# Transposing the dense stages of an encoder trunk: the residual stream as channels by tokens, weights stationary

## The chip, the cores and the metric

The kernel runs on one core of a Trainium2 chip, as one program. The metric is the device time of one execution in microseconds (us). Three runs of the kernel before took 1546.14, 1547.98 and 1548.44 us. A profiled execution took 1544.88 us. In names used below, PE is the matmul engine, PEld its weight load, DVE the vector engine, ACT the activation engine, POOL the GpSimd engine, and SP the engine that issues most transfers.

## What is computed

Two layers work on a stream x of 1024 tokens by 1024 channels in float32. Each layer normalises x, projects it to queries, keys, values and a gate, mixes tokens (layer 0, mixer A: attention over a neighbourhood of a 16 x 64 grid; layer 1, mixer B: attention over all tokens, 16 query heads and 4 key heads, with rotary positions), multiplies by the gate and projects back. Then a second input p is projected and added under a gate:

```python
for i in range(DEPTH):
    h = rms_norm(x, norm_g[i])
    ...
        y = mixer_a(h, a_w_in[j], a_rpb[j], a_w_out[j])
    ...
    x = x + y
    g = jax.nn.sigmoid(rms_norm(x, ple_norm_g[i]) @ ple_w_gate[i])
    x = x + g * (p[i] @ ple_w_proj[i])
return rms_norm(x, final_norm_g)
```

`rms_norm(x, g)` is x times a factor per token, 1/sqrt(mean(x^2) + eps), times a gain g per channel. A mixer ends with `(o * silu(gate)) @ w_out`.

## The kernel before

**Stages.** The program runs mixer A, dense stage 0, mixer B and dense stage 1. A dense stage (`dense_phase(l)`) has two passes. The pass "out" is the output projection plus residual; the pass "ple" is the gate projection, tanh, product with the projected p and residual. In dense stage 1 the pass "ple" ends with the final norm and the store of the result.

**Three products for one.** Every float32 operand is kept as a high part and a low part of a reduced format, and each product is three matmuls (`split3`, all recorded at L317 through `mm`): high by high, high by low, low by high. The activations of the current stage are in `HTh` and `HTl`, as [channel in chunk, token tile, channel chunk, token]: 128 partitions are channels, so they can be either operand of a matmul. There are 8 token tiles of 128 tokens (`NT`) and 8 channel chunks of 128 (`KC`).

**Orientation.** `proj_T` makes an output of channels by tokens: the weight block is stationary, HTh/HTl move with 512 tokens. The mixers use it for queries, keys and gates in A and for gates in B. `proj_N` makes tokens by channels: a token tile of HTh/HTl is stationary and the weights move. Mixer B uses it with 256 columns for q, k and v, and the dense passes use it with 512 columns. A dense pass goes over two halves of the output channels (`hf`), and in each over the 8 token tiles: 24 matmuls of 128x512 to one tile and half, issued as two parts of 12. The very last tile of the last pass is made in two halves of 256 columns.

**Norm and turn.** The residual stream is in eight tiles `X[t]`, tokens by channels. After each half, ACT squares the tile with a running sum (L1282, L1291). When the second half of two tiles is there, `norms` makes the factor (DVE L411, POOL's power L325) and multiplies the tile by factor and gain (DVE L421, 1024 wide). `to_ht` then transposes the product on PE, in groups of four 128x128 transposes into a PSUM bank (L427), and ACT and DVE copy it into HTh and HTl (L428, L429). These groups wait in a list `pend` and one is issued between two parts of 12 matmuls; the last ones of dense stage 0 are issued in mixer B's opening, between its first projections (`pre` in `mixer_b`). In the final pass `norms` writes the result, which SP stores (L1299, L1302).

**Weights.** `Weights` is a queue of units of 128 x 1024 elements. SP loads a unit into one of two staging tiles (L205), ACT writes its high part (L220) and DVE its low part (L221). `pulse` or `WQ.pump` moves it one step after each part: a unit is split at the earliest 3 steps after its load was issued, and the next load is issued at the earliest 3 steps after a split. A dense pass uses eight units, four for each half of the channels; the first half's come from pool 1 (`wp1`, four slots), the second half's from pool 2 (`wp2`, four slots). A unit holds two of the 8 input chunks for 512 output channels. `hold` keeps the staging tiles free while the last normalised tiles use them.

**Order in the mixers.** `mix` interleaves attention steps with projection parts by given costs, and two lists of postponed work (`post`, `later`) tick with it. In mixer B all projections share one PSUM bank after the opening (`pd`, one buffer). Its gate leaves PSUM by an ACT copy (L523); mixer A's gate leaves by a DVE product with `R`, the norm factor per token spread over all partitions (L525), since A's activations are x times gain without the factor. The projected p (`pp_items`, L548) goes to memory in the mixers and comes back in the pass "ple" (`load_pp`, L1258).

## Time and profile before

| | us |
|---|---|
| runs shown | 1546.14, 1547.98, 1548.44 |
| profiled execution | 1544.88 |
| its span, first to last instruction | 1543.1 |
| mixer A with start-up | 0 to 524.8 |
| dense stage 0 | 524.8 to 713.6 |
| mixer B, opening and attention | 713.6 to 1351.3 |
| dense stage 1 to its last matmul | 1351.3 to 1535.6 |
| rest | 1535.6 to 1543.1 |

A line of the profile names the source line, the engine, the operation, output<-inputs by tile name and their shapes, then "x" and the count; behind the bar are the busy time, the mean duration of one in ns, and the idle time before them with what ended it. The duration of a matmul is from its start to its modelled end and overlaps the next one, so the pace is read from starts or from a whole stretch. In the chain of waits a line gives start, length, engine, tile and line.

### The profile page before, as it was taken

The page shows a single profiled execution, that of the slowest core. Times are in us where ns is not written, and L with a number is a line of the kernel's source. Part 1 is how long each engine was busy: PE and PEld are TensorE (multiplying, and loading weights), DVE is VectorE, ACT ScalarE, POOL GpSimd, SP SyncE. Part 2 cuts the span into 40 slices and gives each one's busy share as a digit, 9 for nine tenths or more (in the row PEclk, how much of TensorE's full clock was granted, in tenths as well). Part 3 has the DMA queues.
Part 4 walks back from the last instruction along what each step waited for, and adds up shares of the span by engine and source line. Part 5 has one row for each costly group of instructions (what it writes and reads, how often), then busy time and mean ns, then how long its engine had stood idle before and what let it go on. Part 6 is the DMA issues. An engine that isn't in the chain of part 4 may idle for free.

```text
span 1543.1 us, 24012 instructions
## 1 busy us (share of the span) xinstructions
PE 1513.8 (98%) x9016; PEld 1324.3 (86%) x9016; DVE 963.5 (62%) x1638; ACT 847.5 (55%) x1696; POOL 350.6 (23%) x468
## 2 busy tenths in 40 slices
PE   8999999999999999999999999999999999999998
PEld 8789888988988788888988889989899888788886
DVE  4675676566576435556867776677777877624533
ACT  7564555455466423333467676767767767622422
POOL 1231232223122010000432233545041300000124
PEclk9999999999999999999999999999999999999999
DMA  7211312221124961232210111102111213651213
GB/s 300 79 61 47 96 50 67 68 73 60 62 78 124 352 220 44 89 130 79 85 36 22 39 60 41 51 25 69 40 31 42 76 46 118 225 200 55 71 59 130
DMA packets 85635, 138.97 MB, mean 90 GB/s; under 512 B 12816, under 2 KB 49808, under 8 KB 85520
## 3 DMA queue, kind: packets, MB, share of 16 engines
q1 hardware_dynamic: 80912, 122.77, 24.0%
q10 hardware_dynamic: 4608, 14.68, 2.7%
q8 instruction: 71, 1.16, 0.3%
q14 instruction: 44, 0.36, 0.1%
HBM read 104.80 MB, written 32.62 MB: 89 GB/s over the span
## 4 chain that ended last, share of the span: by engine, by line
PE 84%; DVE 6%; ACT 5%; issue 3%; DMA 1%; POOL 1%; ACTq 0%; POOLq 0%; SPq 0%; DVEq 0%
PE d L317 54%; PE o L317 10%; PE s L317 9%; PE t L1105 6%; PE t L686 2%; DVE PTl L1108 1%; PE t L427 1%; DVE mn L1089 1%; ACT PTh L1107 1%; DVE wl L221 1%; ACT P L1095 1%; ACT wh L220 1%; POOL xn L416 1%; PE t L1059 0%; DMA ppD<-G 0%
## 5 line engine op out<-in xcount | busy, mean ns | idle before, releaser
L317 PE MATMUL d<-wh,HTh 128*128 128x256 f32 (+1 forms) x1064 | 358.7, 341 | 5.3 <-ACT wh L232 2.7
L317 PE MATMUL d<-wh,HTl 128*128 128x256 f32 (+1 forms) x1064 | 352.2, 335 | 0.0
L317 PE MATMUL d<-wl,HTh 128*128 128x256 f32 (+1 forms) x1064 | 352.1, 335 | 0.0
L1108 DVE TENSOR_TENSOR PTl<-t,PTh 128x512 fp32r<-128x512 f32 x256 | 164.4, 683 | 124.1 <-ACT PTh L1107 123.6
L317 PEld LDWEIGHTS d<-wh,HTh 128*128 128x128 f32 x1064 | 200.0, 190 | 28.5 <-ACT wh L232 3.0
L317 PEld LDWEIGHTS d<-wl,HTh 128*128 128x128 f32 x1064 | 200.0, 190 | 21.4
L317 PEld LDWEIGHTS d<-wh,HTl 128*128 128x128 f32 x1064 | 199.8, 190 | 21.6
L317 PE MATMUL d<-HTh,wh 128*128 128x512 f32 x504 | 205.7, 408 | 0.0
L317 PE MATMUL d<-HTh,wl 128*128 128x512 f32 x504 | 198.7, 394 | 0.0
L317 PE MATMUL d<-HTl,wh 128*128 128x512 f32 x504 | 197.7, 392 | 0.0
L1095 ACT ACTIVATE P<-s,mn 128x1024 f32<-128x1024 f32 x128 | 142.8, 1115 | 58.2 <-DVE mn L1089 57.5
L1107 ACT ACTIVATE PTh<-t 128x512 fp32r<-128x512 f32 x256 | 139.9, 594 | 43.5 <-PE t L1105 42.5
L1089 DVE TENSOR_REDUCE mn<-s 128x1 f32<-128x1024 f32 x128 | 154.8, 1209 | 11.7 <-PE s L317 11.6
L1105 PE MATMUL t<-ident,P 128*128 128x128 f32 x1024 | 137.4, 275 | 6.7 <-DVE PTl L1108 4.9
L1105 PEld LDWEIGHTS t<-ident,P 128*128 128x128 f32 x1024 | 114.7, 141 | 22.5 <-DVE PTl L1108 16.6
L317 PE MATMUL s<-KA,QS 128*128 128x512 f32 (+2 forms) x384 | 133.7, 402 | 0.0
L221 DVE TENSOR_TENSOR wl<-wstage,wh 128x1024 fp32r<-128x1024 f32 x86 | 107.5, 1255 | 26.7 <-ACT wh L220 25.7
L317 PE MATMUL s<-KB,QS 128*128 128x512 f32 (+2 forms) x384 | 121.6, 371 | 0.0
L317 PE MATMUL o<-PTh,V 128*128 128x256 f32 (+2 forms) x672 | 118.8, 288 | 2.4 <-ACT P L1095 1.1
L317 PE MATMUL o<-PTl,V 128*128 128x256 f32 (+2 forms) x672 | 118.7, 288 | 0.3 <-DVE PTl L690 0.3
L317 PEld LDWEIGHTS d<-HTh,wl 128*128 128x128 f32 x504 | 94.6, 188 | 21.5
L690 DVE TENSOR_TENSOR PTl<-t,PTh 128x384 fp32r<-128x384 f32 (+1 forms) x128 | 66.7, 521 | 65.2 <-ACT PTh L689 63.8
(172 smaller groups left out, 2486.9 us busy)
## 6 DMA issues: line engine op xcount, KB each, us to landing
wstage<-in_wts SPq DMA_DIRECT2D x92, 512.0 KB
X<-in_x SPq DMA_DIRECT2D x16, 512.0 KB
pp<-ppD SPq DMA_DIRECT2D x32, 256.0 KB
rb<-rD SPq DMA_DIRECT2D x56, 128.0 KB
ppD<-th SPq DMA_DIRECT2D x24, 256.0 KB
XT<-in_xT SPq DMA_DIRECT2D x8, 512.0 KB
xD<-X SPq DMA_DIRECT2D x8, 512.0 KB
X<-xD SPq DMA_DIRECT2D x8, 512.0 KB
```

Of the source, the lines that this page charges most:

```text
L220: act.activation(hi, s, AF.Copy)
L221: self.rest = lambda: dve.tensor_tensor(lo, s, hi, ALU.subtract)
L317: pe.matmul(ps, a, b, start=first, stop=last, skip_group_check=True)
L416: pool.tensor_scalar(xns[i][:, :512], xts[i][:, :512], r[:, i:i + 1], None, op0=ALU.mult)
L427: pe.transpose(ps[:, k], xn[:, (4 * c + k) * 128:(4 * c + k + 1) * 128], ident)
L686: pe.transpose(ps[:, i], sp[:, i * 128:(i + 1) * 128], ident)
L690: dve.tensor_tensor(PTl[:, sl], ps[:, :m], PTh[:, sl], ALU.subtract)
L1089: dve.tensor_reduce(mn, ps, axis=AX.X, op=ALU.min)
L1095: act.activation(p, ps, AF.Exp, bias=mn, scale=-1.0, accum_out=RS[h, hf][:, t:t + 1])
L1105: pe.transpose(ps[:, i], p[:, k * 128:(k + 1) * 128], ident)
L1107: act.activation(PTh[:, ks, c], ps, AF.Copy)
L1108: dve.tensor_tensor(PTl[:, ks, c], ps, PTh[:, ks, c], ALU.subtract)
```

## The change

The residual stream is kept transposed, as two tiles `XR[hf]` of [channel in chunk, channel chunk, 512 tokens], loaded from the transposed input (dense stage 0) or from the transposed copy in memory (dense stage 1). Both dense passes become weight-stationary: a unit of weights now holds all 8 input chunks for one chunk of 128 output channels, four chunks from pool 1 and four from pool 2, and a pass runs over groups of tokens (0 to 511 and 512 to 1023; in the last pass 512, 256 and 256 tokens) and in each over the 8 output chunks, 24 matmuls each, in two parts of 12. The units of a pass are released in its last token group.

The tiles for the next stage are made by `put`: HTh and HTl are written from the residual by ACT and DVE with the gain as a scalar per partition, without the norm factor. The factor goes in later: the gate is multiplied by `RG` as it leaves PSUM, mixer B's gate by `R` on DVE, and mixer B's q, k and v by `rt` as the ACT copy's scale. For the factor the squares of eight chunks are added up on POOL (`acc`), `norm` transposes them on PE and sums along the free axis, POOL takes the power, and `turn` spreads it over partitions by four more transposes. The pieces wait in a list `rest`, one popped after each part of the next group; the last ones run in mixer B's opening. The last 256 tokens end in `end`. The projected p is made transposed too. In mixer A, `put`, `roots` and `spread` replace local functions of the same work.

```diff
...
-        for hf in range(2):
-            names += [("out", l, hf, u) for u in range(4)]
-            names += [("ple", l, hf, u) for u in range(4)]
-            names += [("pp", l, hf)]
+        names += [("out", l, c) for c in range(8)]
+        names += [("ple", l, c) for c in range(8)]
+        names += [("pp", l, hf) for hf in range(2)]
...
+    GN = glob.tile([128, 5, 8], F32, name="GN")
+    rt = glob.tile([128, 8], F32, name="rt")
+    R = glob.tile([128, 1024], F32, name="R")
...
-                if key == self.hold:
-                    return
...
-            for hf in range(2):
-                q.extend([((n, l, hf, u), 1 + hf) for u in range(4)])
+            q.extend([((n, l, c), 1 + c // 4) for c in range(8)])
...
-    def to_ht(pt, t, xn, cs=(0, 1)):
-        for c in cs:
-            ps = pt.tile([128, 4, 128], F32, name="t")
-            for k in range(4):
-                pe.transpose(ps[:, k], xn[:, (4 * c + k) * 128:(4 * c + k + 1) * 128], ident)
-            act.activation(HTh[:, t, 4 * c:4 * c + 4], ps, AF.Copy)
-            dve.tensor_tensor(HTl[:, t, 4 * c:4 * c + 4], ps, HTh[:, t, 4 * c:4 * c + 4], ALU.subtract)
+    def put(src, gi, hf, k, eng=None):
+        ts = slice(4 * hf, 4 * hf + 4)
+        src = src.rearrange("p (t c) -> p t c", t=4)
+        g = GN[:, gi, k:k + 1]
+        act.activation(HTh[:, ts, k, :], src, AF.Copy, scale=g)
+        dve.scalar_tensor_tensor(HTl[:, ts, k, :], src, g, HTh[:, ts, k, :], op0=ALU.mult, op1=ALU.subtract)
+
+    def roots(ms, dst):
+        dve.tensor_scalar(ms, ms, 1.0 / D, EPS, op0=ALU.mult, op1=ALU.add)
+        pool.tensor_tensor(dst, ms, neghalf[:, 0:dst.shape[1]], ALU.pow)
+
+    def spread(ps, r):
+        for i in range(r.shape[1]):
+            pe.transpose(ps[:, i], r[:, i:i + 1].to_broadcast([128, 128]), ident)
...
-            if R is None:
-                act.activation(G, ps, AF.Copy)
-            else:
-                dve.tensor_tensor(G, ps, R[:, hf * 512:(hf + 1) * 512], ALU.mult)
+            dve.tensor_tensor(G, ps, R[:, hf * 512:(hf + 1) * 512], ALU.mult)
...
+                        c = slice(u * 512 + cc * 128, u * 512 + (cc + 1) * 128)
+                        s = slice(th * 512, (th + 1) * 512)
+                        split3(ps, wh[:, c], wl[:, c], ph[:, s], pl[:, s], u == 0, u == 1)
...
+                    act.activation(o, ps, AF.Copy, scale=0.5)
+                    post.add(DP, lambda: sync.dma_start(ppD[l][4 * hf + cc, :, th * 512:(th + 1) * 512], o))
...
-                        act.activation(raw, ps, AF.Copy)
+                        act.activation(raw, ps, AF.Copy, scale=rt[:, t:t + 1])
...
-                if i >= 2 and i % 2 == 0 and pend:
-                    to_ht(psT, *pend.pop(0))
-                if not pend:
-                    WQ.hold = None
                 d[0]()
+                for _ in range(2 if i < 2 else 1):
+                    if pend:
+                        pend.pop(0)(lambda: psT.tile([128, 4, 128], F32, name="t"))
                 pulse()
+            assert not pend
...
+            wp2 = es.enter_context(tc.tile_pool(name=f"wp2{l}", bufs=WSLOTS))
+            XR = [es.enter_context(tc.tile_pool(name=f"xr{hf}", bufs=1)).tile([128, 8, 512], F32, name=f"XR{hf}") for hf in range(2)]
             one = es.enter_context(tc.tile_pool(name="done", bufs=1))
             sb = es.enter_context(tc.tile_pool(name="dsb", bufs=2))
-            ps_d = es.enter_context(tc.tile_pool(name="dps", bufs=4, space=PSUM))
-            ps_t = es.enter_context(tc.tile_pool(name="dpt", bufs=4, space=PSUM))
-            wp2 = es.enter_context(tc.tile_pool(name=f"wp2{l}", bufs=WSLOTS))
-            X = [one.tile([128, D], F32, name=f"X{t}") for t in range(NT)]
+            ps_d = es.enter_context(tc.tile_pool(name="dps", bufs=6, space=PSUM))
+            ps_t = es.enter_context(tc.tile_pool(name="dpt", bufs=2, space=PSUM))
+            rg = one.tile([128, 8], F32, name="rg")
+            RG = one.tile([128, 1024], F32, name="RG")
             WQ.alloc[2] = lambda: [wp2.tile([128, 1024], F32R, name=f"w{c}2") for c in "hl"]
             WQ.cap[2] = WSLOTS
-            for u in range(4):
-                WQ.get(("out", l, 0, u))
-            xs = x if l == 0 else xD
-            g1 = load_gain(sb, 2 * l + 1, 2)
-            g2 = load_gain(sb, 2 * l + 2, 2)
-            pend = []
+            for c in range(4):
+                WQ.get(("out", l, c))
+            xs = xT if l == 0 else xD
+            soon = Later()
...
+            def load_x(hf, c):
+                cs = slice(hf * 512, hf * 512 + 512)
+                sync.dma_start(XR[hf][:, c], xs[c, :, cs])
+
+            def sums(acc, n, ms, talloc):
+                ps = talloc()
+                for i in range(n):
+                    pe.transpose(ps[:, i], acc[:, i * 128:(i + 1) * 128], ident)
+                dve.reduce_sum(ms, ps[:, :n], axis=AX.X)
+
+            def take(r, dst, talloc):
+                n = r.shape[1]
+                ps = talloc()
+                spread(ps, r)
+                act.activation(dst, ps[:, :n].rearrange("p t c -> p (t c)"), AF.Copy)
+
+            rest = []
+            def group(kind, ta, tb, final, to, gi):
+                n = tb - ta
+                w = n * 128
+                hf = ta // 4
+                cols = slice(ta * 128, tb * 128)
+                tail = final and tb == NT
+                acc = glob.tile([128, 512], F32, name="acc", bufs=2)[:, :w]
...
+                def square(c):
+                    xr = X[:, c]
+                    if c == 0:
+                        act.activation(acc, xr, AF.Square)
+                        return
+                    sq = sb.tile([128, 512], F32, name="sq")[:, :w]
+                    act.activation(sq, xr, AF.Square)
+                    if tail and c == 7:
+                        return sq
+                    pool.tensor_tensor(acc, acc, sq, ALU.add)
+
+                def evac(c, ps):
+                    xr = X[:, c]
+                    if kind == "out":
+                        dve.tensor_tensor(xr, ps, xr, ALU.add)
+                        soon.add(2, lambda: square(c))
+                        return
+                    th = sb.tile([128, 512], F32, name="th")[:, :w]
+                    dve.tensor_tensor(th, ps, RG[:, cols], ALU.mult)
+                    act.activation(th, th, AF.Tanh, scale=0.5)
+
+                    def gated():
+                        dve.scalar_tensor_tensor(th, th, 1.0, PP[c], op0=ALU.add, op1=ALU.mult)
+                        dve.tensor_tensor(xr, th, xr, ALU.add)
+                        if l == 0:
+                            sync.dma_start(xD[c, :, cols], xr)
+                        if tail and c == 7:
+                            end(square(c))
+                            return
+                        square(c)
+                        if final:
+                            soon.add(1, lambda: act.activation(xr, xr, AF.Copy, scale=GN[:, 4, c:c + 1]))
+                    if tail and c == 7:
+                        soon.flush()
+                        gated()
+                    else:
+                        soon.add(2, gated)
...
+                def end(sq):
+                    ps = talloc()
+                    for i in range(n):
+                        pe.transpose(ps[:, i], acc[:, i * 128:(i + 1) * 128], ident)
+                    for i in range(n):
+                        pe.transpose(ps[:, n + i], sq[:, i * 128:(i + 1) * 128], ident)
+                    dve.reduce_sum(ms, ps.rearrange("p (s t) c -> p t s c", s=2), axis=AX.XY)
+                    xr = X[:, 7]
+                    act.activation(xr, xr, AF.Copy, scale=GN[:, 4, 7:8])
+                    roots(ms, rt[:, ta:tb])
+                    ps = talloc()
+                    spread(ps, rt[:, ta:tb])
+                    rr = ps[:, :n].rearrange("p t c -> p (t c)")
+                    act.activation(R[:, cols], rr, AF.Copy)
+                    for a, b, q in ((0, 3, sync), (3, 6, act)):
+                        dve.tensor_tensor(X[:, a:b], X[:, a:b], rr[:, None].to_broadcast([128, b - a, w]), ALU.mult)
+                        q.dma_start(out[a:b, :, cols].rearrange("c p t -> p c t"), X[:, a:b])
+                    pool.tensor_tensor(X[:, 6:8], X[:, 6:8], R[:, cols][:, None].to_broadcast([128, 2, w]), ALU.mult)
+                    sync.dma_start(out[6:8, :, cols].rearrange("c p t -> p c t"), X[:, 6:8])
+
+                def norm(talloc, ta=ta, tb=tb, acc=acc, n=n, ms=ms, to=to):
+                    sums(acc, n, ms, talloc)
+                    roots(ms, to[0][:, ta:tb])
+
+                def turn(talloc, ta=ta, tb=tb, cols=cols, to=to):
+                    take(to[0][:, ta:tb], to[1][:, cols], talloc)
...
+                parts = [(c, i) for c in range(8) for i in range(2)]
+                if kind == "out" and ta == 0:
+                    parts = [(c, 0) for c in range(4)] + [(c, 1) for c in range(4)] + parts[8:]
+                    load_x(0, 0)
+                    load_x(0, 1)
+                load_pp(0)
+                load_pp(1)
+                for m, (c, i) in enumerate(parts):
+                    if kind == "out" and m % 2 == 0:
+                        nx = m // 2 + 2
+                        if nx < 8:
+                            load_x(hf, nx)
+                        elif hf == 0:
+                            load_x(1, nx - 8)
+                    if i == 0:
+                        PS[c] = alloc()[:, :w]
+                    key = (kind, l, c)
+                    wh, wl = WQ.get(key)
+                    for k in range(4 * i, 4 * i + 4):
+                        cw = slice(k * 128, (k + 1) * 128)
+                        split3(PS[c], wh[:, cw], wl[:, cw], HTh[:, ta:tb, k, :], HTl[:, ta:tb, k, :], k == 0, k == KC - 1)
+                    if i == 1:
+                        if tb == NT:
+                            WQ.done(key)
+                        evac(c, PS.pop(c))
+                        load_pp(c + 2)
+                    if tail and c == 7 and i == 1:
+                        break
+                    WQ.pump()
+                    soon.tick()
+                    if rest:
+                        rest.pop(0)(talloc)
+                    if l == 0 and kind == "out" and ta == 0 and m == 9:
+                        rope_tables(sb)
+                if tail:
+                    return
+                if not final:
+                    for c in range(8):
+                        rest.append(lambda talloc, c=c, hf=hf, gi=gi: put(XR[hf][:, c], gi, hf, c))
+                    rest.insert(5, norm)
+                    rest.append(turn)
+                else:
+                    rest.extend([lambda talloc: None, lambda talloc: None, norm, lambda talloc: None, turn, lambda talloc, f=store: f()])
...
-                sq = sb.tile([128, 2, NT], F32, name="sq")
-                gt = g1 if kind == "out" else g2
-                for hf in range(2):
-                    cs = slice(hf * 512, (hf + 1) * 512)
-                    keys = [(kind, l, hf, u) for u in range(4)]
-                    parts = []
-                    PP = {}
-
-                    def gated(t, ps, w):
-                        xt = X[t][:, cs][:, w]
-                        th = sb.tile([128, 512], F32, name="th")[:, w]
-                        act.activation(th, ps, AF.Tanh, scale=0.5)
-                        dve.scalar_tensor_tensor(th, th, 1.0, PP[t][:, w], op0=ALU.add, op1=ALU.mult)
-                        dve.scalar_tensor_tensor(xt, th, 0.5, xt, op0=ALU.mult, op1=ALU.add)
-
-                    for t in range(NT):
-                        def evac(ps, t=t):
-                            if kind == "out":
-                                xt = X[t][:, cs]
...
-                        norms(sb, sq, [g[0] for g in grp], [g[1] for g in grp], [X[g[0]] for g in grp], gt, final)
...
-                            pend += [(clock[0] + 3, u, xn, (c,)) for u, xn in grp for c in range(2)]
+                to = (rg, RG) if kind == "out" else (rt, R)
+                gi = 2 * l + (1 if kind == "out" else 2)
+                groups = [(0, 4), (4, 6), (6, 8)] if final else [(0, 4), (4, 8)]
+                for ta, tb in groups:
+                    group(kind, ta, tb, final, to, gi)
+            soon.flush()
             WQ.cap[2] = 0
-            return [p[1:] for p in pend]
+            return rest
...
```

216 lines of the change are left out of this document (63 added, 153 removed).

## The prediction

> **What bounds the kernel now.** I read the busy times and the chain that ended last first, then busy times by stage, then the chain and single instructions inside the dense stages.
>
> ```profile
> PE 1513.8 (98%) x9016; PEld 1324.3 (86%) x9016; DVE 963.5 (62%) x1638; ACT 847.5 (55%) x1696; POOL 350.6 (23%) x468
> PE 84%; DVE 6%; ACT 5%; issue 3%; DMA 1%; POOL 1%; ACTq 0%; POOLq 0%; SPq 0%; DVEq 0%
> ```
>
> TensorE sets the end. Busy time by stage, as mixer A's end, dense 0, mixer B's opening, mixer B's attention, dense 1 and the tail follow one another (columns: length, then PE, PEld, DVE, ACT, POOL busy, clock, DMA share, GB/s):
>
> ```profile
> 524.80:713.60 188.80, 188.59 (x872) 154.33 (x872) 91.87 (x118) 63.61 (x124) 10.39 (x11) 1.00 0.39 134
> 713.60:762.20 48.60, 47.53 (x395) 47.05 (x396) 36.02 (x106) 22.78 (x63) 16.16 (x19) 1.00 0.24 75
> 762.20:1351.30 589.10, 577.49 (x3909) 518.19 (x3909) 427.46 (x609) 414.12 (x767) 167.34 (x230) 1.00 0.19 61
> 1351.30:1535.60 184.30, 184.28 (x856) 151.57 (x856) 76.09 (x106) 53.42 (x108) 32.45 (x26) 1.00 0.29 102
> 1535.60:1543.10 7.50, 0.04 (x1) 0.00 (x0) 1.76 (x4) 1.83 (x4) 1.17 (x2) 0.63 0.36 140
> ```
>
> In both dense stages PE never waits (0.2 us idle in 373), while DVE is below 50%. So every instruction taken off PE there is time, work added on ACT, DVE and POOL is covered while those have slack, and 7.5 us after the last matmul are a serial tail.
>
> **Transposes removed.** L427 turns each normalised token tile, four 128x128 transposes to a group.
>
> ```profile
> L427 PE MATMUL t<-ident,xn 128*128 128x128 f32 x176 | 26.3, 272 | 0.0
> L427 PE MATMUL t<-ident,wstage 128*128 128x128 f32 x16 | 2.4, 272 | 0.0
> ...
> 588.21 0.44 PE t L427 x4
> 588.64 2.80 PE d L317 x12
> 591.44 0.44 PE t L427 x4
> ...
> 724.25 0.44 PE t L427 x4
> 724.69 2.88 PE o L317 x24
> ```
>
> A group costs the path 0.44 us. There are 48 groups (176 and 16 transposes, over four; the next two kinds of row are the chain of waits in dense 0 and in mixer B): 16 after each out pass and 16 after dense 0's gate pass, six of which fall into mixer B's opening. 48 x 0.44 = **-21.1**, of which -2.6 in mixer B. The squares, gains and factors that go with them lay under PE's 2.8 us per part and their removal counts nothing.
>
> **Orientation.** Each 128x512 matmul has the same columns either way. What differs is its spacing.
>
> ```profile
> 37.00 8.20 PE d L317 x36
> ...
> 524.80:568.30 43.50, 43.50 (x192) 36.04 (x193) 1.00 0.76 257
> ```
>
> The first row, of the chain, is mixer A's projection, weights stationary and HTh/HTl moving: 8.20/36 = 0.228 with its first included. The second, of the stages, is the first half of the first out pass, weights moving: 43.50/192 = 0.2266. These agree. But the second half of a pass runs at 2.80/12 = 0.2333 (the row at 588.64). The half that differs takes its moving operand from the second weight pool. In the new form HTh/HTl always moves, so I take 0.2266 throughout: 744 second-half matmuls x 0.0067 = **-5.0**. If the pool costs the same as stationary operand, it is 0; if every matmul took the slower spacing, +5. I take the near row, the same operands at 0.228. Check of the model: dense 0 is 768 x 0.2266 + 384 x 0.0067 + 26 x 0.44 = 188.0 of 188.8.
>
> **256-column groups.** The last gate pass is cut into tokens of 512, 256 and 256. A 256-column matmul takes 2.88/24 = 0.12 (row at 724.69), against 0.113 for half of 0.2266. New: 192 x 0.2266 + 384 x 0.12 = 89.6; old, without the pool effect: 360 x 0.2266 + 48 x 0.12 = 87.3. **+2.3**.
>
> **Transposes added.** `norm` (sums of squares) and `turn` (factor across partitions) are four transposes each for six groups of 512 tokens and one in mixer B, so 14 groups x 0.44 = 6.2, and two half groups for tokens 512 to 767 of the end at about 0.3 (between 0.22 and 0.44). They are popped parts after what they read. The last square of a gate group is added some 4.8 us after its last matmul (DVE 0.69, tanh 0.6, DVE 1.4, square 0.6, POOL about 1.4); `norm` follows that matmul by six parts of 2.7, and `turn` follows `norm` by four, which covers a power (0.70 in a row further down). Only in the last pass are there three short parts, 24 x 0.12 / 2 x 3 = 4.3: PE waits 0.5. Without the cover each group would pay 5. Together **+7.3**.
>
> **Work moved on the other engines.** Per output chunk (5.4 us of PE): out has one DVE addition, a square on ACT, an addition on POOL; gates have three DVE operations (one by RG), tanh and square. With `put` and half a weight split DVE needs at most 3 x 0.69 + 0.75 + 0.6 = 3.4 of 5.4 us, ACT about 2.4, POOL 1.4. This counts nothing, PE covers it, and six PSUM banks let it lag; uncovered it would be some 2 us a chunk.
>
> ```profile
> L1239 DVE TENSOR_TENSOR X<-d,X 128x512 f32<-128x512 f32 x32 | 22.0, 690 | 71.9 <-PE d L317 57.0 <-DMA X<-in_x 14.9
> L738 DVE SCALAR_TENSOR_TENSOR HTl<-XT,g,HTh 128x512 fp32r<-128x512 f32 x16 | 11.1, 745 | 8.3 <-ACT HTh L737 8.2
> ...
> 506.19 1.06 ACT wh L220
> 507.28 1.24 DVE wl L221
> 508.53 5.86 DMA wstage<-in_wts
> ```
>
> Weights: one unit now serves one output chunk, needed whole at its first matmul. c2 at the start of dense 0 is wanted 5.4 us after the start, when its low part has just been written (the split after the final head): **+0.2**, at most 1. Later units: stepping the queue's counters (age 3, lag 3, a pulse per part), out c4 to c7 split after parts 2, 5, 8, 11 and are wanted at 8, 10, 12, 14; the gate's c0 to c7 all come two parts or more early. Counted 0. SP's queue loses four gain loads (512 KB each) and gets residual loads of half the size, ahead of the same weight loads; it gets no later.
>
> **Mixer B.** `put` frees its opening of transposes, and the DVE order (eight puts of 0.7, four rotations, one sum) ends put 7 about 13 us in, wanted at 14.9: no stall, little room. Gates now leave PSUM on DVE, through one bank.
>
> ```profile
> L523 ACT ACTIVATE G<-d 128x512 f32<-128x512 f32 x15 | 9.0, 600 | 15.7 <-PE d L317 15.6
> L525 DVE TENSOR_TENSOR G<-d,R 128x512 f32<-128x512 f32 x16 | 10.8, 677 | 1.0 <-PE d L317 0.9
> L1089 DVE TENSOR_REDUCE mn<-s 128x1 f32<-128x1024 f32 x128 | 154.8, 1209 | 11.7 <-PE s L317 11.6
> L1108 DVE TENSOR_TENSOR PTl<-t,PTh 128x512 fp32r<-128x512 f32 x256 | 164.4, 683 | 124.1 <-ACT PTh L1107 123.6
> ...
> PE d L317 <- ACT th L1027: 0.6, 1, 0.6
> ```
>
> Sixteen times 0.68 move onto an engine busy 73%, behind a reduction of 1.21. Queued behind the new wait are that reduction and PTl, for which PE waits. Between -0.6 (the old wait of PE on L1027 as mixer B opens) and +5; **+1.0**, as the same form in mixer A (L525) kept nobody waiting.
>
> **Tail.**
>
> ```profile
> 1535.36 0.28 PE L317 MATMUL d<-wh,HTl 128*128 128x256 f32 x1
> 1535.68 0.38 ACT L1231 ACTIVATE th<-d 128x256 f32<-128x256 f32 x1 [2.44 <-PE d L317]
> 1536.10 0.43 DVE L1232 SCALAR_TENSOR_TENSOR th<-th,pp 128x256 f32<-128x256 f32 x1 [0.50 <-ACT th L1231]
> 1537.82 0.16 DVE L411 SCALAR_TENSOR_TENSOR stn<-sq 128x1 f32<-128x1 f32 x1 [0.84 <-ACT xn L1291]
> 1538.67 0.75 DVE L419 SCALAR_TENSOR_TENSOR xn<-X,stn,gain 128x512 f32<-128x512 f32 x1 [0.69 <-POOL stn L325]
> 1539.44 0.33 SPq L1299 DMA_DIRECT2D out<-xn  x1
> ...
> GB/s 0 0 0 0 0 0 0 0 0 155 354 376 399 354 421 443 354 377 377 399 354 354 399 399 155 0 0 0 0 0 0 0 0 0 0 0 0 0 0 0
> ...
> L325 POOL TENSOR_TENSOR stn<-stn,neghalf 128x2 f32<-128x2 f32 x12 | 8.4, 698 | 303.4 <-DVE stn L411 303.4
> L936 DVE TENSOR_REDUCE ss<-t 128x4 f32<-128x256 f32 x32 | 13.1, 408 | 3.4 <-ACT t L935 3.1
> L221 DVE TENSOR_TENSOR wl<-wstage,wh 128x1024 fp32r<-128x1024 f32 x86 | 107.5, 1255 | 26.7 <-ACT wh L220 25.7 <-DMA rD<-r8T 0.5
> ```
>
> Now 1535.64 to 1543.1 is 7.5. New: DVE 0.43, tanh 0.38, DVE 2 x 0.43, square 0.4, handovers 0.25: 2.3. Transposes 0.44, a 512-wide sum (between 0.41 and 1.21) 0.65, scaling 0.16, power 0.70, handovers 0.25: 4.5. Two transposes 0.4, a 768-wide product (between 0.69 and 1.25) 1.0: 5.9. Then the stores: 512 KB took 3.66 from issue to end now; 1 MB adds 1.4 at the 375 GB/s of the row above, some 0.5 more if its 1 KB pieces go slower: 5.1 to 5.6. Together about 11.4, **+3.9** (bounds +1.5 and +7).
>
> **Sum.** -21.1 - 5.0 + 2.3 + 7.3 + 0.2 + 1.0 + 3.9 = -11.4. The profiled execution's 1544.88 (span 1543.1 and 1.8 around it) becomes 1533.5. The runs shown have their median 3.1 above it (1547.98), so I forecast **1536.5** for such a median.
>
> **Rivals.** *The spacing stays*: the second pool slows loads as it slowed moving reads. For it: I know the cause of 0.2333 only by where it occurs. Against: the load (0.19) is shorter than the spacing. Time 1536.5 + 5 = 1541.5.
>
> *POOL holds up DVE*: some 60 additions of squares, each reading two SBUF operands, run beside DVE.
>
> ```profile
> 729.94 0.35 DVE L923 TENSOR_TENSOR t<-th,tab 128x64 f32<-128x64 f32 x2
> ...
> 733.19 1.52 POOL L957 TENSOR_TENSOR qt<-qt,ss 128x128 f32<-128x128 f32 x4
> 733.25 0.78 DVE L923 TENSOR_TENSOR t<-th,tab 128x64 f32<-128x64 f32 x2
> ```
>
> Two equal DVE products took 0.35, and 0.78 beside POOL. In the 256-token groups a chunk has only 2.87 us; DVE has 3 x 0.43 and a store product of 0.65 each 1.4 chunks, 1.8 in all, and doubling what runs beside POOL makes 3.2: a lag of 0.3 x 8 = 2.6 that stands in the tail, and about 1 in mixer B: 1536.5 + 3.6 = 1540. The Trainium skill, "SBUF — State Buffer", section "Who interferes with whom", has this as a lock: a DVE instruction with two SBUF inputs and a GpSimd one that reads SBUF exclude each other, the later blocked till the first ends. By that rule the new `put` (source in SBUF, where the transposed tile was in PSUM) joins those that block; the rows of 733 agree in kind.
>
> *Gate evictions stall PE* (slower than before): in mixer B one PSUM bank serves all projections; each of 16 evictions waits on DVE behind a reduction (1.21) and two PTl (1.3), 2.5 us, which ACT's queue did not impose. It decides from (11.4 + 1.0)/16 = 0.78 us each; at 1.5 us each 1536.5 - 1 + 24 = 1559.5. For it: DVE at 73%. Against: ACT was at 70% and no wait of PE on L523 is listed.
>
> *Weights late* (slower too): eight units stay live until the second token sweep. A late unit costs 5.86 + 1.06 + 1.24 - 5.44 = 2.7; five late units undo the gain, all 14 (the gate's c1 to c7, twice) give 1536.5 + 38 = 1574. Against: the counters above.
>
> *Nothing comes of it*: PE's saving returns as waits on DVE or POOL in mixer B's opening and the tail: 1547. Against: 0.2 us idle in dense.
>
> **Chances.** Forecast 0.62 (own range 1529 to 1540), spacing stays 0.12, POOL 0.08, nothing 0.06, gate evictions 0.07, weights 0.05. Faster by over 0.2% (about what a measurement can tell from no change) 0.82, within 0.06, slower 0.12. The range runs from the best bounds (tail +1.5, mixer -0.6: 1532, less the 3 us by which the profiled execution lay below) to short of no change: 1528 to 1545.
>
> **What would show it.** Right: no L427-like groups of 48, dense 0 at about 177 us and dense 1 at 180 with PE busy throughout, spacing 0.2266 in all halves, 11 us after the last matmul. Wrong: 0.2333 with the second pool's units; PE waiting on DVE G or on a wl; gaps before `norm` or `turn`; a mixer B longer than 638 us. What would overturn it is PE idle in the dense stages, above 5 us.

## The result and the profile after

The changed kernel takes 1558.08 us (1555.67 to 1558.57, four runs), the kernel before 1548.21 beside it (1546.14 to 1549.33): a ratio of 1.0067, interval 1.0052 to 1.0082. It is slower. The forecast was 1536.5, with a range of 1528 to 1545.

The busy times and the chain that ended last, of the changed kernel:

```profile
PE 1505.5 (97%) x9058; PEld 1325.3 (85%) x9058; DVE 996.4 (64%) x1678; ACT 857.6 (55%) x1663; POOL 401.7 (26%) x507
PE 74%; DVE 13%; ACT 8%; issue 3%; DMA 1%; ACTq 0%; POOL 0%; DVEq 0%; SPq 0%; POOLq 0%
```

PE is busy 8 us less than before, half of the 16.5 that the terms on PE come to in the sum (-21.1 - 5.0 + 2.3 + 7.3), and yet the span grew by 10.8. In the chain PE fell from 84% to 74%, while DVE rose from 6% to 13% and ACT from 5% to 8%. The chain is one path through the program, and PE is still busy 97% of the span, so this only says where to look: at what PE waits for on DVE and ACT. Next the stages, dense 0, mixer B and dense 1, each from its first matmul to that of the next, dense 1 to its last (columns as in the prediction's stages):

```profile
528.08:712.39 184.31, 179.99 (x792) 148.45 (x793) 93.05 (x112) 61.88 (x92) 44.04 (x33) 0.98 0.39 128
712.39:1355.77 643.38, 627.73 (x4288) 565.68 (x4288) 474.33 (x730) 433.65 (x815) 186.67 (x251) 1.00 0.19 61
1355.77:1541.49 185.72, 180.87 (x988) 157.09 (x988) 92.94 (x129) 66.95 (x118) 45.77 (x40) 1.00 0.29 95
```

| us | before | prediction | after |
|---|---|---|---|
| start of dense 0 | 524.8 | 525.0 | 528.1 |
| dense 0 | 188.9 | 177 | 184.3 |
| mixer B | 637.7 | 637 | 643.4 |
| dense 1 | 184.3 | 180 | 185.7 |
| tail | 7.5 | 11.4 | 12.4 |

The 177 and 180 are the prediction's own roundings. Taken stage by stage, its terms give 177.4 and 180.9, and with these the column adds up to the span that its sum gave, 1543.1 - 11.4 = 1531.7. In the two dense stages PE now stands idle for 4.3 and 4.9 us (184.31 - 179.99 and 185.72 - 180.87), where it was 0.2 in both together before: this is the sign that the prediction had named as overturning it.

The table of waits says where PE stood (columns: who waited for whom, us in total, times, longest):

```profile
PE t L1074 <- DVE PTl L1077: 5.9, 6, 1.6
PE d L316 <- issue: 4.7, 1, 4.7
PE d L316 <- ACT sq L1216: 4.3, 1, 4.3
PE t L1184 <- POOL acc L1219: 3.4, 1, 3.4
...
PE d L316 <- DVE wl L222: 1.5, 1, 1.5
...
PE d L316 <- DVE G L502: 0.2, 1, 0.2
```

Two single waits of 4.7 and 4.3 us stand at the two ends of dense 0, one of 3.4 in the last pass. Before, the longest wait at these places was 1.0. In order of time, the start of dense 0 in the changed kernel (start, duration, instruction, and in brackets what ended the idle time before it):

```profile
523.80 0.60 ACT L525 ACTIVATE G<-d 128x512 f32<-128x512 f32 x1 [0.27 <-ACT th L525]
527.29 0.69 DVE L476 TENSOR_TENSOR Y<-Y,t 128x512 f32<-128x512 f32 x1
528.08 0.76 PE L316 MATMUL d<-HTh,wh 128*128 128x512 f32 x1 [4.66 <-issue]
528.64 0.63 PE L316 MATMUL d<-HTl,wh 128*128 128x512 f32 x1
529.07 0.63 PE L316 MATMUL d<-HTh,wl 128*128 128x512 f32 x1
```

PE starts 0.1 us after DVE ends the mixer's last product, Y times the turned factor, which reads a PSUM bank of mixer A; the eviction that used to release the dense stage (ACT, 524.4) was long done. And the first matmuls are 0.43 apart, not 0.227. The end of dense 0:

```profile
707.68 0.39 PE L316 MATMUL d<-HTh,wl 128*128 128x512 f32 x1
708.15 0.68 DVE L1228 TENSOR_TENSOR th<-d,RG 128x512 f32<-128x512 f32 x1
708.33 0.63 ACT L1216 ACTIVATE sq<-XR 128x512 f32<-128x512 f32 x1 [1.54 <-DVE XR L1233]
709.10 1.27 POOL L1219 TENSOR_TENSOR acc<-acc,sq 128x512 f32<-128x512 f32 x1 [2.43 <-ACT sq L1216]
709.53 1.38 DVE L1232 SCALAR_TENSOR_TENSOR th<-th,pp 128x512 f32<-128x512 f32 x1 [0.70 <-ACT th L1229]
711.56 0.68 DVE L1228 TENSOR_TENSOR th<-d,RG 128x512 f32<-128x512 f32 x1
712.39 0.55 PE L316 MATMUL d<-wh,HTh 128*128 128x256 f32 x1 [4.32 <-ACT sq L1216]
```

The last group's matmuls end at 708.07, but its product with RG runs from 711.56 to 712.24: DVE is 3.5 us late, still with the chunk before. Mixer B's first matmul follows at 712.39. The view of waits puts this down to the square on ACT; the order of time suggests the product. The granted clock, that is the share of its full speed at which PE's clock ran, by windows (length, busy times, then the clock in the last column but two):

```profile
527.15:533.97 6.82, 5.89 (x14) 4.69 (x15) 3.68 (x5) 1.57 (x2) 0.00 (x0) 0.50 0.65 219
533.97:539.86 5.89, 5.89 (x27) 4.86 (x27) 1.22 (x1) 1.15 (x2) 0.00 (x0) 1.00 0.95 313
711.47:718.29 6.82, 5.90 (x28) 5.93 (x29) 4.72 (x6) 3.38 (x6) 2.58 (x2) 0.50 0.43 169
718.28:724.17 5.89, 5.89 (x51) 5.89 (x51) 4.57 (x14) 4.27 (x12) 0.25 (x1) 1.00 0.11 32
```

At each of the two gaps the clock is half for 6.8 us, of which 5.9 lie behind the gap. In 5.89 us PE starts 14 matmuls where it then starts 27, and 27 or 28 where it then starts 51: each gap costs some 2.8 us beyond its length.

### The profile page after: what moved, and what is told of

Same layout as the page of the kernel before. It is cut to its first block, busy times and chain, and to the rows that moved or that the text cites. A ratio compares the mean times of both kernels' runs of the same rounds, so it can differ in the third digit from the quotient of the medians.

```text
span 1553.9 us, 24232 instructions
## 1 busy us (share of the span) xinstructions
PE 1505.5 (97%) x9058; PEld 1325.3 (85%) x9058; DVE 996.4 (64%) x1678; ACT 857.6 (55%) x1663; POOL 401.7 (26%) x507
## 4 chain that ended last, share of the span: by engine, by line
PE 74%; DVE 13%; ACT 8%; issue 3%; DMA 1%; ACTq 0%; POOL 0%; DVEq 0%; SPq 0%; POOLq 0%
PE d L316 47%; PE o L316 10%; PE s L316 8%; PE t L1074 5%; DVE PTl L1077 2%; PE t L663 2%; DVE mn L1058 2%; DVE wl L222 2%; DVE th L1232 1%; ACT PTh L1076 1%; DVE HTl L401 1%; DVE XR L1233 1%; ACT wh L221 1%; ACT HTh L400 1%; ACT P L1064 1%
## 5 line engine op out<-in xcount | busy, mean ns | idle before, releaser
L316 PE MATMUL d<-HTh,wh 128*128 128x512 f32 (+1 forms) x1080 | 419.0, 388 | 5.6 <-issue 4.7
L316 PE MATMUL d<-HTh,wl 128*128 128x512 f32 (+1 forms) x1080 | 409.7, 379 | 1.5 <-DVE wl L222 1.5
L316 PE MATMUL d<-HTl,wh 128*128 128x512 f32 (+1 forms) x1080 | 409.3, 379 | 0.0
L316 PEld LDWEIGHTS d<-HTh,wl 128*128 128x128 f32 x1080 | 203.9, 189 | 41.2 <-DVE wl L222 1.9
L316 PEld LDWEIGHTS d<-HTh,wh 128*128 128x128 f32 x1080 | 204.2, 189 | 37.1 <-issue 5.1
L316 PEld LDWEIGHTS d<-HTl,wh 128*128 128x128 f32 x1080 | 204.5, 189 | 30.2
L1219 POOL TENSOR_TENSOR acc<-acc,sq 128x512 f32<-128x512 f32 (+1 forms) x62 | 75.6, 1219 | 368.5 <-ACT sq L1216 368.5
L316 PE MATMUL d<-wh,HTh 128*128 128x256 f32 x544 | 153.9, 290 | 7.2 <-ACT sq L1216 4.3
L316 PE MATMUL d<-wl,HTh 128*128 128x256 f32 x544 | 151.2, 285 | 0.0
L316 PE MATMUL d<-wh,HTl 128*128 128x256 f32 x544 | 151.1, 285 | 0.0
```

Of the source, the lines that this page charges most:

```text
L316: pe.matmul(ps, a, b, start=first, stop=last, skip_group_check=True)
L1219: pool.tensor_tensor(acc, acc, sq, ALU.add)
```

## The experiments

**The two gaps.** Theory A: both gaps are hand-overs of PSUM, the first because the change widened the dense pool from four banks to six, the second because DVE runs late, and the half clock follows from the gaps. The rivals are landings of HTh and HTl, too much work on DVE, the squares on ACT, and another cause of the clock. All four kernels start from the changed one.

*e1: four banks.* The mixer's pools d, s, t and o hold two banks each, in this order. Six dense banks reach over t, four do not.

```
-            ps_d = ... tc.tile_pool(name="dps", bufs=6, space=PSUM)
+            ps_d = ... tc.tile_pool(name="dps", bufs=4, space=PSUM)
```

> The changed kernel with four PSUM banks for the dense groups where it has six (the other two for turning stay). Theory A, hand-over of banks: with six banks the dense pool lies over the mixer's transpose banks, so its first matmul waits for DVE's last product Y<-Y,t (ends at 527.98 in the profile of the changed kernel, the matmul starts at 528.08), and the granted clock falls to half behind the gap. With four banks the first matmul goes at about 524.5, as in the kernel before (524.79), without a gap above 1.2 us and without the half clock: 3.5 + 3.4 = about 7 us less, 1551. Rival B, landing: the first matmul waits for the token tiles of HTh and HTl, which it now needs four at a time: it stays at 528.1 and the time at 1558. Rival C, too few banks: DVE runs up to 8 us late in the gated pass, and four banks let PE wait for it: more than 1558.

Measured: 1552.28 us, ratio to the kernel before 1.0036 (1.0022 to 1.0049). PE's wait at this place, in e1:

```profile
525.04 0.49 PE L316 MATMUL d<-HTh,wh 128*128 128x512 f32 x1 [1.02 <-ACT G L525]
```

The wait is the old one again, on ACT, 1.0 us, and no half clock follows: A holds, the landings fall (B), and no new wait on DVE's products appears (C). Against the changed kernel's 1.0067 the saving is 0.31%, 4.8 us; it is short of 7, in part since a half clock turned up elsewhere (last section).

*e2: the DVE half of `put` one half-group later.*

```
-        dve.scalar_tensor_tensor(HTl[:, ts, k, :], src, g, HTh[:, ts, k, :], ...)
+        low = lambda: dve.scalar_tensor_tensor(HTl[:, ts, k, :], src, g, HTh[:, ts, k, :], ...)
+        if when:            # the dense stage's list "soon"; none in mixer B
+            when.add(1, low)
+        else:
+            low()
```

> The changed kernel; in the dense stages the DVE half of each put is queued one half-group later than the ACT half, so that DVE does not stand 1.3 us behind ACT each time. Theory A, DVE is late: the product with RG of the last group starts 3.5 us after its matmuls because DVE is held in order behind ACT, and the first matmul of mixer B waits for that product. Then the product follows the last matmul within 0.5 us, the gap before mixer B shrinks from 4.3 to about 1 us, the half clock behind it (3.4 us) goes, and the 3.4 us before the sums of the last pass shrink too: 1558 - 3.3 - 3.4 - 2.5 = 1549. Rival B, DVE has too much work, not a wrong order: the gap stays above 3 us and the time within 2 us of 1558. Rival C, the opening of mixer B waits for the squares on ACT, as the view of waits names it: the gap stays above 3 us although the product is early.

Measured: 1546.83 us, 1.0004 (0.9995 to 1.0013). DVE's groups of dense 0 (busy us and mean ns, then idle before them), first of the changed kernel, then of e2:

```profile
L401 DVE SCALAR_TENSOR_TENSOR HTl<-XR,GN,HTh 128x512 fp32r<-128x512 f32 x24 | 23.7, 990 | 29.5 <-ACT HTh L400 29.5
L1228 DVE TENSOR_TENSOR th<-d,RG 128x512 f32<-128x512 f32 x16 | 10.9, 682 | 0.9 <-PE d L316 0.9
```

```profile
L401 DVE SCALAR_TENSOR_TENSOR HTl<-XR,GN,HTh 128x512 fp32r<-128x512 f32 x24 | 19.8, 829 | 0.2
L1233 DVE TENSOR_TENSOR th<-d,RG 128x512 f32<-128x512 f32 x16 | 11.0, 689 | 26.4 <-PE d L316 26.4
```

and the end of dense 0 in e2 in order of time:

```profile
708.05 0.69 DVE L1233 TENSOR_TENSOR th<-d,RG 128x512 f32<-128x512 f32 x1 [2.63 <-PE d L316]
708.89 0.36 PE L316 MATMUL d<-wh,HTh 128*128 128x256 f32 x1 [0.88 <-DVE th L1233]
```

DVE's 29.5 us of standing behind ACT are gone with the order of two instructions, and now the product waits for PE, 26.4 us where it was 0.9, as it should. The last one follows its matmul at once, the gap is 0.88 us, and its row names DVE's product. Theory A holds; too much work (B) and the squares (C) fall. The 3.4 us before `norm` in the last pass shrank as well, to 0.7. By the ratios e2 saves 0.63%, 9.7 us; 9 were foreseen. Two things in e2's profile are not the edit's work and about cancel: the half clock behind the first gap lasts 3.4 us (529.5 to 532.9) and not 6.8, which is worth some 1.2 us by the 2.8 above, and dense 0 starts 1.0 us later (529.13).

*e3: filler.* The waits stay; PE gets 36 transposes that nothing reads.

```
+            if l == 0:              # ahead of dense 0's first group, and again behind its last
+                ps = talloc()
+                for i in range(36):
+                    pe.transpose(ps[:, i % 4], ident, ident)
```

> The changed kernel with 36 transposes of the identity into a bank that nothing reads, put on PE at the end of mixer A and at the end of dense 0, some 4 us each, where PE has gaps of 4.7 and 4.3 us. Theory A: the waits stay (first matmuls still at about 528.1 and 712 less what the first one saves), but PE is not idle, the granted clock stays 1.0 and matmuls of 512 columns stand at 0.227 from the start in place of 0.427: 2 x 3.4 = 6.8 us less, 1551. Rival B: the half clock has another cause than the idle PE (the transfers, the other engines' load): it stays, and the time is 1558. Rival C: only what is long idle counts and 4 us of filler leave the gaps too long: one of the two drops stays, 1554.6.

Measured: 1552.89 us, 1.0040 (1.0027 to 1.0053).

```profile
524.33 4.15 PE L1196 MATMUL t<-ident 128*128 128x128 f32 x36 [0.32 <-DVE Y L423]
528.67 0.47 PE L316 MATMUL d<-HTh,wh 128*128 128x512 f32 x1 [0.18 <-issue]
```

and, as a window, the 5.89 us behind it:

```profile
528.67:534.56 5.89, 5.89 (x26) 4.90 (x27) 2.96 (x3) 1.52 (x2) 0.00 (x0) 1.00 0.51 168
```

The first matmul still goes at 528.7, but at full clock, with the DMA engines busy for a share of 0.51; mixer B too opens at full clock (641.2 us long, not 643.4). So the idle PE is the cause of the half clock, and the transfers are not. By the ratios 0.27% or 4.2 us came back with both waits in place. That is less than 6.8: the filler itself ends 0.6 us late at dense 0, and in e3's profile, as in e1's, a half clock followed the 3.4 us gap of the last pass, which it did not in the changed kernel's.

*e4: e1 and e2 together.*

> e1 and e2 together: four banks for the dense groups, and the DVE half of each put one half-group later. Theory A: the two gaps are independent, so the savings add: 7 + 9 = 16 us less, about 1542, faster than the kernel before by 0.4%. Rival B: four banks and a late DVE hold PE inside the gated passes, where six did not: waits on DVE th turn up among PE's, and the time is 1546 or more. Rival C: the time that the two gaps take returns in mixer B (PTl on DVE): 1548 to 1552.

Measured: 1541.66 us, 0.9966 (0.9954 to 0.9979): 1.0% or 15.6 us less than the changed kernel, where 16 was expected. Its stages:

```profile
525.21:703.61 178.40, 177.52 (x792) 146.42 (x793) 87.51 (x116) 63.68 (x94) 47.16 (x34) 1.00 0.43 144
703.61:1343.62 640.01, 624.91 (x4288) 563.13 (x4289) 472.09 (x730) 433.29 (x815) 185.09 (x250) 1.00 0.19 60
1343.62:1526.64 183.02, 180.82 (x988) 157.08 (x988) 87.13 (x129) 67.25 (x118) 47.54 (x40) 1.00 0.30 97
```

With these two edits the change is a gain. What is left against the sum of the prediction is 7.4 us: the start of dense 0 +0.2, dense 0 +1.0, mixer B +3.0, dense 1 +2.1, the tail +1.1.

**The rest of dense 1.** *e5: earlier weights* (`WQ.age = WQ.lag = 2` inside the dense stages of e4, where both are 3).

> e4 (1541.7) with the weights of the dense stages split two half-groups after their load and after one another, where it was three. Theory A: PE's one wait for the low part of a weight unit in dense 1 (1.5 us at 1396 in the profile of the changed kernel) comes from the split being queued too late on DVE, behind a sum that itself waits for PE; earlier by one half-group it goes: 1.5 us less, 1540.2, dense 1 181.5 us in place of 183.0. Rival B: the unit is late because its load is (the XR loads share SP's queue): the wait stays, 1541.7. Rival C: the earlier splits push other work of DVE and ACT back, and PE waits elsewhere: 1542 to 1545.

Measured: 1540.45 us, 0.9955 (0.9940 to 0.9970); PE's wait for a weight unit is gone, and dense 1 takes 181.3 where e4 has 183.0. By the profile theory A holds; the times alone do not show it, since the intervals of e4 and e5 overlap. *e7: the first group of mixer B into the bank of o*, over which no pool of the dense stage lies (on e4, `pro[1] % 2 == 1` for `== 0` at both places).

> e4 (1541.7) with the first group of mixer B written to the bank of the pool o, over which no pool of the dense stage lies, and the second to the pool d, the other way round from e4. Theory A, hand-over by pools: the first group needs nobody's release and starts 0.3 us after the last dense matmul in place of 0.88; the second waits less than 0.2 us, as 2.7 us have gone by: 0.9 us less, 1540.8. Rival B: the first group waits for something else (its weights, HTh): the 0.88 us stay. In either case within 0.1% of e4.

Measured: 1543.60 us, 0.9970 (0.9959 to 0.9981). The first group indeed waits for nobody:

```profile
704.20 0.39 PE L316 MATMUL d<-HTh,wh 128*128 128x512 f32 x1
...
705.34 0.39 PE L316 MATMUL d<-HTh,wl 128*128 128x512 f32 x1
705.56 0.28 PE L316 MATMUL o<-wh,HTh 128*128 128x256 f32 x1
```

So the wait is for what lies under the new tile's pool. But no time was gained. Dense 0 is 1.1 us shorter (177.3) and mixer B 1.6 longer (641.6; e2 to e5, which share one mixer B, have 640.0 to 641.2). And dense 0 starts 3.0 us later than in e4 (528.2 against 525.2), which lies ahead of all that the edit touches; the last section says what stands there. *e8: e5, e7 and the last pass's sums one half-group later* (a third empty entry ahead of `norm` in `rest`).

> e4 with e5's earlier weights, e7's first bank, and the sums of the last pass queued one half-group later (PE waits 0.73 us for POOL's acc there in e4). Theory A: 1.5 + 0.9 + 0.5 = 2.9 us less than e4, 1538.8, faster than the kernel before by about 0.5%. Rival: the parts do not add, since the tail's chain on DVE and ACT ends the kernel: 1540 to 1542.

Measured: 1539.96 us, 0.9953 (0.9940 to 0.9966). Dense 1 takes 180.2, close to what the prediction gave it, with no wait before `norm`. The total is only 0.5 us below e5's, but by stages the parts are there: against e5 dense 0 is 1.0 us shorter (177.4), mixer B 0.2 and dense 1 1.1. What hides them is that dense 0 starts 2.3 us later (527.6 against 525.3), as in e7.

**Mixer B.** e4 reaches its first transposed product 3.2 us sooner than the kernel before (70.35 against 73.55 us after the stage's first matmul) and then loses 5.5 us over the rest:

```profile
787.19:1351.32 564.13, 553.86 (x3774) 497.70 (x3772) 408.81 (x582) 400.15 (x744) 156.53 (x218) 1.00 0.19 61
```

```profile
773.96:1343.62 569.66, 556.02 (x3774) 497.39 (x3773) 417.71 (x596) 394.27 (x730) 156.46 (x218) 1.00 0.19 60
```

The first row is a window of the kernel before, the second of e4: the same 3774 matmuls, 9 us more on DVE. *e6: the gates leave PSUM on ACT, and POOL multiplies* (on e4, in mixer B alone; in mixer A the old lines stay).

```
-            dve.tensor_tensor(G, ps, R[...], ALU.mult)
-            act.activation(th, G, AF.Tanh, scale=0.5)
+                act.activation(G, ps, AF.Copy)
+                pool.tensor_tensor(G, G, R[...], ALU.mult)
+                post.add(1, lambda: act.activation(th, G, AF.Tanh, scale=0.5))
```

> e4 (1541.7) with mixer B's gates taken out of PSUM by ACT (a copy), multiplied by R on POOL and given to the hyperbolic tangent one item later, so that DVE does nothing for them but the fold. Theory A: DVE's 16 products of 0.69 us are what lengthens PE's waits for PTl in mixer B from 6.2 us before to 8.1: they fall back to about 6.2 and the time by 2 us, 1539.7. Rival B: mixer B is as long as it is for other reasons (the order of its opening): the waits stay, 1541.7. Rival C: ACT, which sets the waits for PTh and P, is lengthened by 16 x 0.6 us, or POOL's products hold DVE up: 1543 or more.

Measured: 1546.49 us, 0.9990 (0.9980 to 1.0000). Mixer B is 646.7 us long; PE's waits for PTl are 10.8 us where e4 has 8.1, one of them 2.8 us. Behind that one the clock is half for 6.8 us (771.7 to 778.5). So of the 6.7 us by which mixer B is longer than in e4, 2.7 are longer waits for PTl and some 2.8 this half clock, an estimate by what the same length cost in the changed kernel. C is what came: taking the product off DVE this way is no remedy. Two smaller edits on e5 part DVE's load from ACT's wait. *e9: the tangent one item later* and *e10: the last step on POOL*:

```
-            act.activation(th, G, AF.Tanh, scale=0.5)
+            post.add(1, tanh)                      # e9, mixer B alone; the fold one item later too
...
-                dve.scalar_tensor_tensor(G, th, 1.0, G, op0=ALU.add, op1=ALU.mult)
+                    pool.tensor_tensor(th, th, G, ALU.mult)     # e10, mixer B alone
+                    pool.tensor_tensor(G, G, th, ALU.add)
```

> e5 (1540.4) with the tangent of mixer B's gates queued on ACT one item after their product on DVE, where it was queued at once. Question: e4 opens mixer B 3.2 us sooner than the kernel before, but loses 5.5 us over the rest of it, in eight steps of 0.3 to 1.0 us. Theory A: the new form of the gates, a DVE product that the tangent waits for, holds ACT in order as the puts held DVE; PTh and P on ACT are late by that, and PTl behind them. Then mixer B shrinks from 641.0 to about 638 us and the time to 1537.5. Rival B, DVE has 32 more operations there (0.69 us each, of which some stand ahead of PTl): the wait of ACT costs nothing, 1540.4. Rival C: the tangent one item later delays PTh: 1541 or more.

> e5 (1540.4) with the last step of mixer B's gates, (tangent + 1) x gate, done by two operations on POOL in place of one on DVE; product and tangent stay as they are. DVE then has as many operations for the gates as in the kernel before. Theory A of e9: ACT waits for the product as ever, so the time stays within 1 us of 1540.4. Rival B of e9, the number of DVE operations: PE's waits for PTl fall from 8.3 to about 6 us and the time to 1538. Rival C: POOL's operations slow DVE's next to them, or are late for Y: 1542 or more.

Measured: e9 1538.02 us, 0.9941 (0.9926 to 0.9956), mixer B 636.8 us; e10 1537.57 us, 0.9946 (0.9931 to 0.9960), mixer B 639.0. In e5 mixer B is 641.0. By the profiles ACT's wait for the product counts 4.2 us and DVE's operations 2.0, where the profiles of e2 to e5, with one and the same mixer B, differ by 1.2. PE's waits for PTl fall from 8.3 us in e5 to 6.4 in e9 and 6.0 in e10 (where PE waits 1.2 us for POOL's new operations instead), so A and B each seem to hold a part, B's hardly more than that difference. By the ratios it is 0.14% and 0.09%, with intervals that overlap e5's: the times of single edits do not show it. *e11: e5, e9, e10 and e8's later sums.*

> e5 with both edits of mixer B's gates (e9's later tangent, e10's last step on POOL) and the sums of the last pass one half-group later (e8). Theory: the two edits of the gates act on two queues, so what they save adds, as far as PE's waits for PTl and PTh reach (in e9 5.8 + 0.6 us of PTl are left, in e10 5.6 + 0.4): mixer B 636 us, dense 1 180.5, and 1540.4 - 4 to 5 - 1 = 1535 to 1536, which is the time that the prediction gave for the changed kernel. Rival: both edits remove the same waits: mixer B stays at e9's 637 us, and the time at 1537 to 1538.

Measured: 1534.87 us (1533.63 to 1535.70), 0.9922 (0.9909 to 0.9936), the best of all: 0.8% faster than the kernel before, 1.5% faster than the changed one, and clear of e5's interval, so its edits together do count. Its mixer B and dense 1, then PE's waits for PTl in mixer B, first in the kernel before, then in e11:

```profile
704.49:1340.20 635.71, 623.79 (x4289) 563.18 (x4289) 465.85 (x714) 434.03 (x815) 230.31 (x282) 1.00 0.19 61
1340.20:1520.37 180.17, 180.17 (x988) 157.15 (x988) 87.91 (x129) 67.77 (x118) 48.33 (x39) 1.00 0.30 97
```

```profile
PE t L1105 <- DVE PTl L1108: 4.9, 5, 1.6
PE t L1059 <- DVE PTl L1108: 1.3, 3, 0.9
```

```profile
PE t L1087 <- DVE PTl L1090: 5.7, 5, 1.5
...
PE t L1041 <- DVE PTl L1090: 0.6, 3, 0.2
```

6.2 us before and 6.3 now, where e4 has 8.1.

## Why the prediction was wrong, step by step

**What bounds the kernel** was right: PE, with the others covered. **Transposes removed** was right: dense 0 has 792 matmuls, 768 and 24 transposes, where it had 872, and mixer B 16 fewer (24 gone, 8 added). **Orientation** was right: in the last chunk, whose weights come from the second pool, e7's matmuls are (705.34 - 704.20)/5 = 0.228 apart (the first and the last of six in the rows shown at e7), so the rival "the spacing stays" falls. In e4 PE is busy 177.5 us in dense 0, where the prediction's terms give 177.4.

**The step that failed** is "Work moved on the other engines ... This counts nothing, PE covers it, and six PSUM banks let it lag". Its load was right: DVE needs 93 of dense 0's 184 us. But it added up durations, and DVE takes its instructions in order. In each `put` it stood behind ACT, 29.5 us in dense 0 or 1.2 a `put`; the row of L738 that the prediction shows has such a wait already, 8.2 us for 16 of them. So DVE fell behind, and a product whose matmuls were done then stood in the queue behind the chunk before: the last one started a round trip of product, tangent and two more operations after that chunk's product, 711.56 - 708.15 = 3.4 us. Six banks did let it lag, so no wait shows inside the pass; the lag is paid where the pass ends. There it cost 4.3 us at mixer B, of which 0.9 is left in e2, 2.8 of half clock, and 2.7 of the 3.4 before `norm` (queueing the sums later, in e8, took the rest); **transposes added** had put that wait at 0.5. e2 shows this part by itself.

And the six banks themselves were the second failure, in **the start of dense 0**, +0.2 and "at most 1". I looked at c2's low part and not at what the new pool lies over. It cost 3.3 us of waiting and 2.8 of half clock; e1 shows it.

Third, no term priced an idle PE beyond its length. The Trainium skill, "TensorE: Matmul & The Clock Gate", section "What's actually happening", says that PE falls back to half clock after an idle window of about 3.4 us and returns after a busy one. The trace agrees, with 0.50 behind idle stretches of 4.3 and 4.7 us, and e3 with 1.00 where they were filled (the last section has stretches where it does not); it was a rule that spoke against this change, once a wait of that length could arise.

Of the rivals, "nothing comes of it" (0.06) came nearest: it has waits on DVE in mixer B's opening. But it had neither the start of dense 0 nor the clock, and so its 1547 is short as well.

**Mixer B**, +1.0 with bounds of -0.6 and +5, was mis-sized: in e4 it is 5.5 us over the body. The opening gave 1.5 back (3.2 us shorter, where the transposes taken and added, -2.6 + 0.9, give 1.7), so the term came out at 4.0 by these profiles. "The same form in mixer A kept nobody waiting" was no ground: DVE is busy 63% of mixer A and 73% of mixer B. e9 and e10 point at ACT's wait for the product and, less clearly, at the number of DVE's operations. The rival "gate evictions stall PE" has the place right and the way wrong: PE's wait for the gate's bank is 0.2 us in all. Put 7 kept nobody waiting.

**Weights**, counted 0: one unit late by 1.5 us. The pulses were counted rightly, but the low part stood on DVE behind a sum that itself waits for PE (the sum starts at 1394.19, the low part at 1394.80); the rival of five late units falls.

**POOL holds up DVE** was there in kind: L1232 takes 1.38 us beside POOL's addition and 0.69 otherwise (the rows of 709.10 and 709.53). The Trainium skill, "SBUF — State Buffer", section "Who interferes with whom", has it for a DVE instruction with two SBUF operands, and the trace agrees in kind. But this product met it only while DVE was late: in the changed kernel its mean in dense 0 is 911 ns, in e4 it is 689:

```profile
L1237 DVE SCALAR_TENSOR_TENSOR th<-th,pp 128x512 f32<-128x512 f32 x15 | 10.3, 689 | 3.5 <-ACT th L1234 3.5
```

**The tail**, 11.4, measured 12.4: the sums to the power came as forecast; missing were ACT's eviction of the factor (0.4) ahead of DVE's products and the second of these (0.9). In return the end comes 4.8 us behind the last product, where the stores had been counted at 5.1 to 5.6.

```profile
1546.89 0.38 ACT L1261 ACTIVATE R<-t 128x256 f32<-128x256 f32 x1 [2.52 <-PE t L409]
1547.31 1.82 DVE L1263 TENSOR_TENSOR XR<-XR,t 128x768 f32<-128x768 f32 x2 [1.98 <-ACT R L1261]
```

With the two gaps taken out and nothing else, e4's span is 1539.1, 7.4 us above the 1531.7 of the sum. e11's span is 1532.3, but e11 also has other gates, weights and sums than the kernel of the prediction. The terms on PE's path were sound; the prediction failed at "counts nothing". That e11 comes so near is partly luck: its dense 0 starts later (526.0) and is longer (178.5), as is its tail (11.9), and its mixer B (635.7) and dense 1 (180.2) are shorter than in the sum.

## What to carry to other kernels

Before you widen a PSUM pool, look at which pools of the closing stage lie under it and who reads them last: in this program the new stage's first matmul waited for that reader. Work on an engine that runs in order is covered by its busy share only if no instruction in its queue stands waiting for another engine; queue the second half of such a pair one step later, and check how late the engine is at the end of each stage, where lag turns into a gap. Price a gap of PE of some 3 us or more at its length and up to 3 us on top: here gaps of 4.7 and 4.3 us cost 2.8 each beyond their length and one of 2.8 (e6) was followed by half clock too, while one of 3.4 in the changed kernel was not. And when two profiles differ, compare them stage by stage: a half clock ahead of what an edit touches can hide what the edit did, as in e7 and e8.

## What the runs showed of the hardware that was not expected

The same wait need not cost the same. The gap of 3.4 us before `norm` was followed by full clock in the changed kernel and by half clock in e1 (windows of the changed kernel over its gap and what follows, then of e1):

```profile
1494.69:1498.08 3.39, 0.00 (x1) 0.01 (x1) 2.63 (x4) 1.55 (x3) 1.26 (x1) 1.00 0.14 41
1498.08:1501.49 3.41, 3.41 (x29) 3.41 (x30) 2.31 (x6) 1.24 (x3) 1.02 (x1) 1.00 0.11 38
```

```profile
1489.41:1494.02 4.61, 1.24 (x11) 1.14 (x11) 3.74 (x6) 1.96 (x4) 1.28 (x2) 1.00 0.10 30
1494.02:1497.43 3.41, 3.41 (x18) 3.41 (x18) 1.73 (x5) 0.82 (x2) 1.02 (x1) 0.50 0.15 38
```

And in e9 the clock fell after a stretch that was never idle for long: 1.85 us busy of 3.41, in several short waits at the end of mixer A.

```profile
518.17:521.58 3.41, 1.85 (x11) 1.32 (x10) 1.59 (x4) 1.65 (x4) 0.00 (x0) 1.00 1.03 412
521.58:525.00 3.42, 3.42 (x13) 2.73 (x12) 0.46 (x2) 1.63 (x3) 0.00 (x0) 0.50 1.02 406
```

The Trainium skill, "TensorE: Matmul & The Clock Gate", section "What's actually happening", calls the window free-running, so equal gaps can fall in it differently. By its rule of a whole idle window of 3.4 us neither e1's gap nor e9's stretch would have been expected to halve the clock: in the last 3.41 us ahead of e1's half clock PE is busy for 1.14. What share of a window has to be idle stays open.

The same half clock explains a good part of the late starts of dense 0. It started between 525.0 and 526.0 in the profiles of six kernels with four banks and between 527.6 and 528.2 in three (e7, e8 and e9), though their instructions up to there are the same. These three, and none of the six, have a half clock of some 3.4 us at the end of mixer A: 0.50 in the row of e9, in e7 from 522.0 to 525.0 and in e8 from 522.5 to 525.5, where e4 has 1.00 from 522.0 to 525.0. Ahead of it PE waits for PTh on ACT, 1.2 to 2.3 us in the three and 0.7 to 1.3 in the six, while ACT issues the loads of HTh and HTl. Why the waits differ between executions was not tried.
